# Moving the low parts of two kinds of weight tiles by 64 bytes, with the retention state updated in place

## The chip, the cores and the metric

One core of a Trainium2 chip runs the whole program. The metric is device time in microseconds (us) of one execution, taken as the median of several runs. Matrix products run on TensorE (PE in the profile, its weight loads PEld), elementwise work on VectorE (DVE) and ScalarE (ACT), a few small steps and some transfers on GpSimd (POOL); the other transfers are issued by SyncE (SP).

## What is computed

One decoder block over 512 tokens of width 1024, in float32. Two mixers work side by side on the normalised input: a chunked retention with 4 heads and a sliding-window attention with 8 heads. Their outputs are gated and merged, and a squared-ReLU MLP of width 4096 follows. Cut to what bears on the change:

```python
h = rmsnorm(x, pre_mix_norm)
q_r, k_r, v_r, g_r, q_s, k_s, v_s, gate_r, gate_s = split(h @ w_in)
# retention: 4 heads, chunks of 128 tokens; kv[n] = k_dec[n].T @ v[n] is 128 x 256
def step(s, kv_n): return chunk_decay * s + kv_n, s      # the state before each chunk
o = decayed(q k^T) v + q_dec @ s_prev                    # then normalised per head
y_r = (silu(g_r) * ret) @ w_ret_out
...
x = x + rmsnorm((sigmoid(gate_r) * y_r + sigmoid(gate_s) * y_s) @ w_out)
x = x + rmsnorm(relu(rmsnorm(x) @ w_up) ** 2 @ w_down)
```

## The kernel before

**Two-part operands.** Every large product is made from operands split in two: `split` writes the high part `hi` on ScalarE (L158, a cast to float32r) and the low part `lo = src - hi` on VectorE (L160). `mm3` then issues three matmuls for one product: high by high (L221), high by low (L222), low by high (L223). In a matmul one operand is loaded as weights (128 columns, the stationary one) while the other streams past it (256 or 512 columns, the moving one). In the text a triple is one `mm3`, and its time is from the start of its L221 to the start of the next triple's L221.

**Where the parts of a weight tile lie.** `place` (L165) hands out the high part as a slice of a tile of 1024 + 64 numbers, four in rotation: with `front=True` from its start, otherwise from its 16th number (64 bytes) on. The low part is a tile of its own, `wlo`, of 1024 numbers, and does not know `front`. The callers with `front=True` are `block_parts` (the q and k weights of retention heads 0 and 2, which are not computed in pairs) and `moving_parts` (the wide weights `w_v` and `w_g` of `wide`). As the pools lay it out in the built program, the starts in SBUF leave these remainders on division by 256 bytes. They are places of tiles, not measurements:

| operands of the triples | moving operand | stationary operand |
|---|---|---|
| `wide` before | `whi` 64, `wlo` 128 | `hT`, `hsum` 64 |
| `wide` after | `whi` 64, `wlo` 64 | `hT`, `hsum` 64 |
| plain retention blocks `pblk<-hT` before | `hT` 64 | `whi` 64, `wlo` 128 |
| plain retention blocks `pblk<-hT` after | `hT` 64 | `whi` 64, `wlo` 64 |
| `ps` (w_out), `yr`, `ys`, `p`, `pblk<-xg`, and the short `p4c`, before and after | 128 | 128 |
| `wino`, `up`, `rpair`, before and after | 64 | 128 |
| `ret_v<-st`, before and after | 64 | 64 |

No matmul other than those of the first two pairs of rows changes its remainders.

**Stages.** After the attention's queries come the q and k of head 0 (`ret_block`, `pblk`), then `wide(w_v)`: seven products of 8 triples each (2 token halves by 4 rows), interleaved with the attention's scores (`swa_s`), transposes (`psd`, `psp`) and values (`pso`). Then the four retention heads: a head's keys and scores, three states (`ret_st`, `ret_states`), the next head's q and k (`pblk` for head 2, a Winograd-like `rpair` for heads 1 and 3), and `ret_values`, in which chunk c needs state c - 1. The last head runs inside `wide(w_g)`, seven products more. Output projections, gates and the MLP follow.

**Retention state.** `ret_states` keeps the running state in a tile `st` of a rotation of two. The first state is a copy by ScalarE (L627), each later one is `prev * decay + kv` on VectorE (L629), written to the other tile, and each is split into a high and a low part by L158 and L160.

**What sets the order.** Each engine runs its own instructions in a fixed order, which a scheduler derives from the order of the code, from what depends on what and from `issue_after`, which holds steps back behind a named one. A tile of a rotation is handed out again once its last reader is done. The `accpool` tile `acc` (4096 numbers in each partition, one in rotation) first holds the two halves of `w_v` that `wide_sums` loads (L698, L700 on SP's queue, L699 on POOL's).

Of the kernel before, what the change touches and what calls it, by code (L numbers as in the profile page):

```python
# [10 lines left out]
F32 = mybir.dt.float32  # L11
F32R = mybir.dt.float32r
# [4 lines left out]
P = 128  # L17
D_MODEL = 1024
SEQ = 512
NT = SEQ // P  # L20
KD = D_MODEL // P
RET_HEADS = 4
RET_DK = 128
RET_DV = 256
# [19 lines left out]
def log_gammas():  # L44
    return np.log(1.0 - np.exp2(-5.0 - np.arange(RET_HEADS, dtype=np.float64)))
# [64 lines left out]
def block_kernel(ctx, tc, x, xT, pre_mix, w_in, w_qk, w_v, w_g, w_gate, w_ret, w_swa, w_out, sinks, post_mix,  # L110
# [6 lines left out]
    stream = ctx.enter_context(tc.tile_pool(name="stream", bufs=4))  # L117
    psum = ctx.enter_context(tc.tile_pool(name="psum", bufs=8, space=PSUM))
    small = ctx.enter_context(tc.tile_pool(name="small", bufs=4))

    def bank(shape, name="ps"):
        return psum.tile(shape, F32, tag="ps", name=name)

    def pad(pool, size, name="pad"):

        pool.tile([P, size // 4], F32, name=name, bufs=1)
# [18 lines left out]

    def rstd_of(sumsq, n, scale):

        ms = small.tile([P, 4], F32, name="ms", bufs=2)
        r = small.tile([P, 4], F32, name="rstd")
        nc.vector.tensor_scalar(ms[:, :n], sumsq, scale, EPS, op0=ALU.mult, op1=ALU.add)  # L150
        nc.gpsimd.tensor_tensor(r[:, :n], ms[:, :n], mhalf[:, :n], op=ALU.pow)
        return r

    last = {}

    def split(hi, lo, src):

        last["hi"] = nc.scalar.copy(hi, src)  # L158
        last["prior"] = last.get("split")
        last["split"] = nc.vector.tensor_tensor(lo, src, f(hi), op=ALU.subtract)  # L160
# [1 line left out]
    def raw_tile(shape):  # L162
        return stream.tile(shape, F32, name="raw", tag="raw", bufs=2)

    def place(shape, front=False):  # L165

        whole = stream.tile([P, 1024 + 64], F32R, name="whi", tag="whi")
        flat = whole[:, :1024] if front else whole[:, 16 : 16 + 1024]
        dims = " ".join("abc"[: len(shape) - 1])
        sizes = {n: shape[i + 1] for i, n in enumerate("abc"[: len(shape) - 1])}  # L170
        hi = flat.rearrange(f"p ({dims}) -> p {dims}", **sizes)
        if "wlo" not in last:
            pad(stream, 64)
            last["wlo"] = True
        return hi, stream.tile(shape, F32R, name="wlo", tag="wlo")

    def parts(src, shape, front=False):
        hi, lo = place(shape, front)
        split(hi, lo, src)
        return hi, lo  # L180

    def load_feature_pair(w, c0):

        nk = w.shape[0] // P
        raw = raw_tile([P, nk, 256])
        nc.sync.dma_start(raw, w[:, c0 : c0 + 256].rearrange("(k p) c -> p k c", p=P))
        return [parts(raw[:, :, b * P : (b + 1) * P], [P, nk, P]) for b in range(2)]
# [8 lines left out]
    def block_parts(raw):  # L196

        return [parts(raw[:, b], [P, KD, P], True) for b in range(2)]
# [19 lines left out]
    def mm3(ps, a, b, first, last, more=False):  # L218

        (ah, al), (bh, bl) = a, b  # L220
        nc.tensor.matmul(ps, ah, bh, start=first, stop=False, skip_group_check=more)  # L221
        nc.tensor.matmul(ps, ah, bl, start=False, stop=False, skip_group_check=more)  # L222
        return nc.tensor.matmul(ps, al, bh, start=False, stop=last, skip_group_check=more)  # L223
# [131 lines left out]
    accpool = ctx.enter_context(tc.tile_pool(name="accpool", bufs=1))  # L355
# [21 lines left out]
    xpool = xctx.enter_context(tc.tile_pool(name="xpool", bufs=1))  # L377
# [46 lines left out]
    def token_factors(t):  # L424

        ss = small.tile([P, 2], F32, name="ss", tag="ss", bufs=2)
        junk = xpool.tile([P, D_MODEL], F32, name="junk")
        last["square"] = nc.scalar.activation(junk, xts[t], AF.Square, accum_out=ss[:, 0:1])
        rstd[t] = rstd_of(ss[:, 0:1], 1, 1.0 / D_MODEL)[:, 0:1]
        diag[t] = xpool.tile([P, P], F32, name="diag", bufs=NT)  # L430
        nc.vector.tensor_scalar(diag[t], ident, rstd[t], None, op0=ALU.mult)
# [28 lines left out]
        return R  # L460

    def half_parts(src):
        hi, lo = place([P, KD, P])
        for i in range(2):
            k = slice(i * KD // 2, (i + 1) * KD // 2)
            split(hi[:, k], lo[:, k], src[:, k])
        return hi, lo

    wq = [half_parts(raw_q[:, :, :P]), parts(raw_q[:, :, P:], [P, KD, P])]
    for t in range(NT):  # L470
        token_factors(t)
# [140 lines left out]
    def ret_states(kd, v, h):  # L612

        decayed = float(np.exp(log_gammas()[h] * P))
        states, prev, pss = [], None, []
        for c in range(NT - 1):
            pss.append(bank([P, RET_DV], "ret_st"))
            mm3(
                pss[c], tuple(a[:, c, :] for a in kd), tuple(a[:, c, :] for a in v), True, True
            )  # L620
        for c in range(NT - 1):
            if c == 1:
                yield states
            st = [rpool.tile([P, RET_DV], F32R, name=f"st{i}", bufs=3) for i in range(2)]
            cur = rpool.tile([P, RET_DV], F32, name="st")
            if prev is None:
                nc.scalar.copy(cur, pss[c])  # L627
            else:
                nc.vector.scalar_tensor_tensor(  # L629
                    cur, prev, decayed, pss[c], op0=ALU.mult, op1=ALU.add  # L630
                )
            split(st[0], st[1], cur)
            states.append(st)
            prev = cur
        yield states
# [173 lines left out]
    rpool = rctx.enter_context(tc.tile_pool(name="rpool", bufs=2, side="right"))  # L809
# [57 lines left out]
    for i in range(3):  # L867
# [4 lines left out]
        if i == 1:  # L872
            rs = dpool.tile([P, 2, 4, P], F32, name="rs1", tag="qs")
# [12 lines left out]
    for h in range(RET_HEADS):  # L886
        if 0 < h < RET_HEADS - 1:
            wqk = load_qk(h + 1)
        with ExitStack() as queue:
            if h and h not in PAIRED:  # L890
                queue.enter_context(tc.issue_after(last["block"].ins))
            v = parts(vg[:, :, h * RET_DV : (h + 1) * RET_DV], [P, NT, RET_DV])
# [209 lines left out]
    for bp in range(KD // 2):  # L1102
# [3 lines left out]
        for b in range(2):  # L1106
            hi = mpool.tile([P, SEQ], F32R, name="mhi", tag="m")
            lo = mpool.tile([P, SEQ], F32R, name="mlo", tag="m")
# [20 lines left out]
    def square_sum(srcs, junk):  # L1129
        ss = small.tile([P, 2], F32, name="ss2", tag="ss", bufs=2)  # L1130
        for i, s in enumerate(srcs):
            c = slice(i * 512, (i + 1) * 512)
            nc.scalar.activation(junk[:, c], s, AF.Square, accum_out=ss[:, i : i + 1])
        nc.vector.tensor_add(ss[:, 0:1], ss[:, 0:1], ss[:, 1:2])
        return rstd_of(ss[:, 0:1], 1, 1.0 / D_MODEL)

    h2 = []
    for half in range(2):
# [11 lines left out]
        with tc.high_priority(offset=CHAIN_AHEAD):  # L1150
            for t in range(2):
# [4 lines left out]
                for n in range(2):  # L1156
                    c = slice(n * 512, (n + 1) * 512)
# [110 lines left out]
    dpool2 = ctx.enter_context(tc.tile_pool(name="dpool2", bufs=1, side="right"))  # L1268
# [92 lines left out]
    fin = ctx.enter_context(tc.tile_pool(name="fin", bufs=2))  # L1361
# [44 lines left out]
    def squares(t, i, src):  # L1406

        w = src.shape[1]
        junk = junks.tile([P, 512], F32, name="junk2")
        ss = fin.tile([P, 1], F32, name="ssf", bufs=6)  # L1410
        nc.scalar.activation(junk[:, :w], src, AF.Square, accum_out=ss)
        ms = fin.tile([P, 1], F32, name="msf", bufs=6)
        rest = EPS if i == 0 else ms0[t][:, 0:1]
        nc.vector.tensor_scalar(ms, ss, 1.0 / D_MODEL, rest, op0=ALU.mult, op1=ALU.add)
        ms0[t] = ms
# [14 lines left out]
    def weigh(n, src):  # L1430
        nc.vector.tensor_tensor(src, src, g_out[:, n * 512 : (n + 1) * 512], op=ALU.mult)


    for tb in range(2):
        nc.scalar.copy(p1c[tb], p1[tb])
        v = fin.tile([P, 512], F32, name="c", bufs=4)
        nc.vector.tensor_tensor(v, p2[tb], p1c[tb], op=ALU.add)
        squares(tb, 0, v)
        weigh(0, v)
        outz[tb] = v  # L1440
        nc.vector.tensor_tensor(p15[tb], p1c[tb], p5[tb], op=ALU.add)
    p6, p3 = banks2("p6"), banks2("p3")
    p7 = None
    rb = {}

    def step_p6(j):
        if j >= T2_DMA:
            nc.vector.tensor_tensor(tch[j], tch[j], rb[j], op=ALU.add)
        a, b = left(j, 1), right(tch[j])
        t_add(tch[j], 1, 0, j)  # L1450

        nc.vector.tensor_tensor(uc[j][:, 1], uc[j][:, 2], uc[j][:, 1], op=ALU.subtract)
        product2(p6, j, a, b)
# [22 lines left out]
    def combine(tb):  # L1476
        nc.vector.tensor_tensor(p15[tb], p6[tb], p15[tb], op=ALU.subtract)
        nc.vector.tensor_tensor(u3[tb], p6[tb], p1c[tb], op=ALU.subtract)
        nc.vector.tensor_tensor(p1c[tb], p3[tb], p15[tb], op=ALU.add)
        squares(tb, 1, p1c[tb])  # L1480
        nc.vector.tensor_tensor(u3[tb], p7[tb], u3[tb], op=ALU.add)
        v = fin.tile([P, 512], F32, name="c", bufs=4)
        nc.vector.tensor_tensor(v, p7[tb], p15[tb], op=ALU.add)
        squares(2 + tb, 0, v)
        outz[2 + tb] = v
# [24 lines left out]
    for i in range(2):  # L1510
        c = slice(i * 256, (i + 1) * 256)
# [9 lines left out]
    junk = junks.tile([P, 512], F32, name="junk2")  # L1521
    ms = fin.tile([P, 1], F32, name="msf", bufs=6)
# [43 lines left out]
```

## Time and profile before

| | |
|---|---|
| median of 3 runs | 713.01 us (712.79 to 713.19) |
| the profiled execution, its own time | 713.18 us |
| its span in the profile | 711.4 us |
| TensorE busy | 703.4 us, 4526 matmuls |
| VectorE, ScalarE, GpSimd busy | 535.4, 431.4, 62.3 us |

TensorE is busy for nearly the whole span, but a busy matmul in these records overlaps the next one: a matmul of 512 columns lasts 0.39 us in its row, and the next starts some 0.23 us after it. What a matmul costs is therefore read from the distance of starts, and over many matmuls, since a row's start is given to 0.01 us.

### The profile page before, as it was taken

To read this page: it belongs to the slowest core of one execution; us is meant where nothing else is said; L and a number is where in the kernel's file an instruction comes from. 1 tells how busy PE (TensorE), PEld (TensorE's weight loads), DVE (VectorE), ACT (ScalarE), POOL (GpSimd) and SP (SyncE) were. 2 spreads that over 40 slices of the span, in tenths; PEclk is the share of its full clock that TensorE was granted. 3 is DMA by queue.
4 is the path that set the end of the run, shared out by engine and by line. 5 is a ranking of instruction groups with operands and counts; after the bars stand their busy time and mean duration, and the time that the engine had idled before them with its cause. 6 is when DMAs were issued, how large, how long until landed. Compare 5 with 4: busy or idle time off the path is not lost.

```text
span 711.4 us, 11459 instructions
## 1 busy us (share of the span) xinstructions
PE 703.4 (99%) x4526; PEld 629.8 (89%) x4526; DVE 535.4 (75%) x801; ACT 431.4 (61%) x734; POOL 62.3 (9%) x78
## 2 busy tenths in 40 slices
PE   9999999999999999999999999999999999999996
PEld 9887889898888999989888999999999888888885
DVE  5699978685975767566945867778777887977797
ACT  6758776566655535435633866766668656655561
POOL 0300100121100000000011100000000100010010
PEclk9999999999999999999999999999999999999999
DMA  9974624876444545553661619777753999798603
GB/s 305 340 191 96 146 56 152 219 170 127 88 149 119 147 120 166 159 150 117 219 256 61 163 45 294 198 195 173 195 148 119 267 290 269 161 214 188 118 1 118
DMA packets 40613, 119.37 MB, mean 168 GB/s; under 512 B 3568, under 2 KB 17008, under 8 KB 34416
## 3 DMA queue, kind: packets, MB, share of 16 engines
q1 hardware_dynamic: 33648, 81.41, 33.0%
q0 software_dynamic: 6768, 37.23, 28.1%
q8 instruction: 35, 0.57, 0.3%
q14 instruction: 18, 0.15, 0.1%
q10 hardware_dynamic: 144, 0.00, 0.0%
HBM read 116.54 MB, written 2.10 MB: 167 GB/s over the span
## 4 chain that ended last, share of the span: by engine, by line
PE 91%; DVE 4%; DMA 2%; issue 1%; ACT 1%; SPq 0%; POOL 0%; DVEq 0%; POOLq 0%; ACTq 0%
PE wino L221 9%; PE wino L223 9%; PE wino L222 9%; PE p L221 5%; PE p L223 5%; PE p L222 5%; PE wide L221 4%; PE wide L222 4%; PE wide L223 4%; PE pblk L223 2%; PE pblk L222 2%; PE pblk L221 2%; PE yr L222 2%; PE ps L222 2%; PE ps L221 2%; PE yr L223 2%
## 5 line engine op out<-in xcount | busy, mean ns | idle before, releaser
L160 DVE TENSOR_TENSOR wlo<-raw,whi 128x1024 fp32r<-128x1024 f32 (+1 forms) x78 | 94.0, 1208 | 37.0 <-ACT whi L158 36.9
L158 ACT CAST whi<-raw 128x1024 fp32r<-128x1024 f32 (+1 forms) x78 | 80.6, 1039 | 19.5 <-PE p L223 4.6
L221 PE MATMUL p<-whi,left 128*128 128x512 f32 x216 | 84.0, 390 | 0.1
L222 PE MATMUL p<-wlo,left 128*128 128x512 f32 x216 | 84.1, 389 | 0.0
L223 PE MATMUL p<-whi,left 128*128 128x512 f32 x216 | 84.0, 390 | 0.0
L223 PEld LDWEIGHTS p<-whi,left 128*128 128x128 f32 x216 | 40.5, 188 | 8.7 <-DVE left L160 0.3
L222 PEld LDWEIGHTS p<-wlo,left 128*128 128x128 f32 x216 | 40.5, 188 | 8.6
L221 PEld LDWEIGHTS p<-whi,left 128*128 128x128 f32 x216 | 40.5, 188 | 8.6 <-ACT left L158 0.5
L158 ACT CAST p<-rs 128x1024 fp32r<-128x1024 f32 x22 | 23.1, 1052 | 36.5 <-DVE rs L275 36.4
L158 ACT CAST left<-uc 128x1024 fp32r<-128x1024 f32 x28 | 29.5, 1052 | 24.5 <-PE p L222 22.7
L160 DVE TENSOR_TENSOR left<-uc,left 128x1024 fp32r<-128x1024 f32 x28 | 34.2, 1221 | 12.3 <-ACT left L158 12.3
L160 DVE TENSOR_TENSOR p<-rs,p 128x1024 fp32r<-128x1024 f32 x22 | 27.0, 1225 | 16.7 <-ACT p L158 16.7
L160 DVE TENSOR_TENSOR wlo<-rs,whi 128x1024 fp32r<-128x1024 f32 x23 | 28.1, 1223 | 13.1 <-ACT whi L158 10.6
L158 ACT CAST whi<-acc 128x1024 fp32r<-128x1024 f32 x20 | 20.5, 1053 | 14.7 <-PE pblk L222 5.6
L221 PE MATMUL wino<-h2s,p 128*128 128x256 f32 x104 | 28.8, 277 | 0.0
L222 PE MATMUL wino<-h2s,p 128*128 128x256 f32 x104 | 28.7, 276 | 0.0
L223 PE MATMUL wino<-h2s,p 128*128 128x256 f32 x104 | 28.7, 276 | 0.0
L221 PE MATMUL wino<-h2c,whi 128*128 128x256 f32 x104 | 28.7, 276 | 0.0
L222 PE MATMUL wino<-h2c,whi 128*128 128x256 f32 x104 | 28.7, 276 | 0.0
L221 PE MATMUL wino<-h2s,whi 128*128 128x256 f32 x104 | 28.7, 276 | 0.0
L222 PE MATMUL wino<-h2s,whi 128*128 128x256 f32 x104 | 28.7, 276 | 0.0
L223 PE MATMUL wino<-h2s,wlo 128*128 128x256 f32 x104 | 28.7, 276 | 0.0
(413 smaller groups left out, 2373.0 us busy)
## 6 DMA issues: line engine op xcount, KB each, us to landing
rs<-in_w_up SPq DMA_DIRECT2D x13, 512.0 KB, 4.4
rs<-in_w_up POOLq DMA_DIRECT2D x13, 512.0 KB, 5.6
raw<-in_w_up SPq DMA_DIRECT2D x13, 512.0 KB, 5.5
tch<-in_w_down POOLq DMA_DIRECT2D x6, 1024.0 KB, 8.4
rd<-in_w_down SPq DMA_DIRECT2D x6, 1024.0 KB, 10.8
raw<-in_w_down POOLq DMA_DIRECT2D x6, 1024.0 KB, 11.5
acc<-in_w_v POOLq DMA_DIRECT2D x4, 1024.0 KB, 8.0
rs<-in_w_gate SPq DMA_DIRECT2D x8, 512.0 KB, 3.8
```

Of the source, the lines that this page charges most:

```text
L158: last["hi"] = nc.scalar.copy(hi, src)
L160: last["split"] = nc.vector.tensor_tensor(lo, src, f(hi), op=ALU.subtract)
L221: nc.tensor.matmul(ps, ah, bh, start=first, stop=False, skip_group_check=more)
L222: nc.tensor.matmul(ps, ah, bl, start=False, stop=False, skip_group_check=more)
L223: return nc.tensor.matmul(ps, al, bh, start=False, stop=last, skip_group_check=more)
```

## The change

`place` now makes one part at a time and is called for the high and for the low part, so that the low parts get tiles of 1024 + 64 numbers in four rotations of their own and obey `front`. Room in SBUF for them comes from four edits: the square's scratch tile `junk` moves from `xpool` into the one `acc` tile; the retention state is one tile for each head that is updated in place; the last products keep two of four `c` tiles in `dpool2` (`c2`); `ms` gets the pool's four tiles in place of two.

```diff
-        ms = small.tile([P, 4], F32, name="ms", bufs=2)
+        ms = small.tile([P, 4], F32, name="ms")
...
-    def place(shape, front=False):
-
-        whole = stream.tile([P, 1024 + 64], F32R, name="whi", tag="whi")
+    def place(name, shape, front=False):
+
+        whole = stream.tile([P, 1024 + 64], F32R, name=name, tag=name)
         flat = whole[:, :1024] if front else whole[:, 16 : 16 + 1024]
...
-        if "wlo" not in last:
-            pad(stream, 64)
-            last["wlo"] = True
-        return hi, stream.tile(shape, F32R, name="wlo", tag="wlo")
...
     def parts(src, shape, front=False):
-        hi, lo = place(shape, front)
+        hi, lo = place("whi", shape, front), place("wlo", shape, front)
         split(hi, lo, src)
...
-        junk = xpool.tile([P, D_MODEL], F32, name="junk")
+        if "junk" not in last:
+            last["junk"] = accpool.tile([P, D_MODEL], F32, name="junk", tag="acc")
+        junk = last["junk"]
...
     def half_parts(src):
-        hi, lo = place([P, KD, P])
+        hi, lo = place("whi", [P, KD, P]), place("wlo", [P, KD, P])
...
             st = [rpool.tile([P, RET_DV], F32R, name=f"st{i}", bufs=3) for i in range(2)]
-            cur = rpool.tile([P, RET_DV], F32, name="st")
+            cur = prev or rpool.tile([P, RET_DV], F32, name="st", bufs=1)
...
-        v = fin.tile([P, 512], F32, name="c", bufs=4)
+        v = fin.tile([P, 512], F32, name="c", bufs=2)
...
+    c2 = dpool2.tile([P, 2, 512], F32, name="c2", tag="rs")
...
-        v = fin.tile([P, 512], F32, name="c", bufs=4)
+        v = c2[:, tb]
```

No instruction is added or removed, and TensorE's order is the same. VectorE's and ScalarE's orders change around the retention states. On VectorE, head 0 (the tile `st` is the running state, `st_1338`, `st_1387` and `st_1393` are the low parts of the three states, `whi` and `wlo` from `vg` are the next head's values) stands before as:

```order
L629 SCALAR_TENSOR_TENSOR st<-st,ret_st 128x256
L160 TENSOR_TENSOR st_1338<-st,st_1337 128x256
L629 SCALAR_TENSOR_TENSOR st<-st,ret_st 128x256
L160 TENSOR_TENSOR swaT<-pso,swaT 128x512
L160 TENSOR_TENSOR st_1387<-st,st_1386 128x256
L160 TENSOR_TENSOR st_1393<-st,st_1392 128x256
L847 TENSOR_TENSOR qk<-rpair,qk 128x256
L848 TENSOR_TENSOR qk<-qk,rpair 128x256
L160 TENSOR_TENSOR wlo<-vg,whi 128x1024
```

and after (lines 2 less; `st_1334`, `st_1383`, `st_1388` are the low parts):

```order
L160 TENSOR_TENSOR st_1334<-st,st_1333 128x256
L627 SCALAR_TENSOR_TENSOR st<-st,ret_st 128x256
L160 TENSOR_TENSOR swaT<-pso,swaT 128x512
L160 TENSOR_TENSOR st_1383<-st,st_1382 128x256
L627 SCALAR_TENSOR_TENSOR st<-st,ret_st 128x256
L845 TENSOR_TENSOR qk<-rpair,qk 128x256
L846 TENSOR_TENSOR qk<-qk,rpair 128x256
L160 TENSOR_TENSOR wlo<-vg,whi 128x1024
L160 TENSOR_TENSOR st_1388<-st,st_1387 128x256
```

Each update of the state now stands behind the split of the state before it, and the third state's low part behind the wide split `wlo<-vg`. On VectorE, head 1 (`rs` and `p` are sums of the weights of head 3) before:

```order
L160 TENSOR_TENSOR st_1555<-st,st_1554 128x256
L629 SCALAR_TENSOR_TENSOR st<-st,ret_st 128x256
L275 TENSOR_TENSOR rs<-rs,raw 128x512
L160 TENSOR_TENSOR st_1561<-st,st_1560 128x256
L160 TENSOR_TENSOR p_1651<-rs,p_1650 128x1024
L160 TENSOR_TENSOR p_1655<-raw,p_1654 128x512
```

and after:

```order
L271 TENSOR_TENSOR rs<-rs,raw 128x512
L160 TENSOR_TENSOR st_1549<-st,st_1548 128x256
L627 SCALAR_TENSOR_TENSOR st<-st,ret_st 128x256
L160 TENSOR_TENSOR p_1643<-rs,p_1642 128x1024
L160 TENSOR_TENSOR st_1554<-st,st_1553 128x256
L160 TENSOR_TENSOR p_1647<-raw,p_1646 128x512
```

Here, too, the third state's low part has moved behind a wide split, that of `rs` into `p`. Heads 2 and 3 show the same move. SP's order is unchanged; its load of `acc` (L698) now waits for the last use of `junk` on ScalarE.

## Rows read from the trace of the kernel before

**Rows 1.** The page: granted clock in 40 slices; chain that ended last, by engine.
```profile
PEclk9999999999999999999999999999999999999999
...
PE 91%; DVE 4%; DMA 2%; issue 1%; ACT 1%; SPq 0%; POOL 0%; DVEq 0%; POOLq 0%; ACTq 0%
```

**Rows 2.** Timeline of PE, `wide` on `w_g`: start us, us, what.
```profile
173.27 0.39 PE L221 MATMUL wide<-whi,hT 128*128 128x512 f32 x1
...
173.97 0.39 PE L221 MATMUL wide<-whi,hT 128*128 128x512 f32 x1
...
174.65 0.40 PE L221 MATMUL wide<-whi,hT 128*128 128x512 f32 x1
...
176.04 0.40 PE L221 MATMUL wide<-whi,hT 128*128 128x512 f32 x1
...
176.75 0.39 PE L221 MATMUL wide<-whi,hT 128*128 128x512 f32 x1
...
201.10 0.39 PE L221 MATMUL ys<-swaT,whi 128*128 128x512 f32 x1
```

**Rows 3.** Timeline of PE, output projection `ps`, first and last start of 56 triples.
```profile
347.13 0.39 PE L221 MATMUL ps<-wo,mhi 128*128 128x512 f32 x1
...
385.21 0.40 PE L221 MATMUL ps<-wo,mhi 128*128 128x512 f32 x1
```

**Rows 4.** Timeline of PE, plain retention blocks of head 0.
```profile
41.16 0.39 PE L221 MATMUL pblk<-hT,whi 128*128 128x512 f32 x1
...
41.62 0.40 PE L223 MATMUL pblk<-hT,wlo 128*128 128x512 f32 x1
41.86 0.39 PE L221 MATMUL pblk<-hT,whi 128*128 128x512 f32 x1
...
51.56 0.39 PE L221 MATMUL pblk<-hT,whi 128*128 128x512 f32 x1
```

**Rows 5.** Timeline of PE, short triples (256 columns) of three stages.
```profile
110.88 0.28 PE L221 MATMUL rpair<-hT,whi 128*128 128x256 f32 x1
...
115.30 0.28 PE L221 MATMUL rpair<-hT,early_qk 128*128 128x256 f32 x1
...
125.23 0.28 PE L221 MATMUL ret_v<-st,qc 128*128 128x256 f32 x1
...
125.59 0.28 PE L221 MATMUL ret_v<-whi,pt 128*128 128x256 f32 x1
...
700.26 0.28 PE L221 MATMUL p4c<-whi,left 128*128 128x256 f32 x1
...
703.86 0.28 PE L221 MATMUL p4c<-whi,left 128*128 128x256 f32 x1
```

**Rows 6.** Timeline of DVE and PE around the third states of heads 0 and 1.
```profile
124.37 1.23 DVE L160 TENSOR_TENSOR wlo<-vg,whi 128x1024 fp32r<-128x1024 f32 x1 [0.20 <-ACT whi L158]
...
126.79 0.28 PE L222 MATMUL ret_v<-st,qc 128*128 128x256 f32 x1
...
139.84 0.42 DVE L160 TENSOR_TENSOR st<-st,st 128x256 fp32r<-128x256 f32 x1
...
141.04 1.22 DVE L160 TENSOR_TENSOR p<-rs,p 128x1024 fp32r<-128x1024 f32 x1 [0.78 <-ACT p L158]
...
142.63 0.28 PE L222 MATMUL ret_v<-st,qc 128*128 128x256 f32 x1
```

**Rows 7.** Timeline of DVE and PE where the attention's probabilities are handed over.
```profile
64.83 1.08 DVE L542 TENSOR_SCALAR s<-s,den 128x128 f32<-128x128 f32 x4
...
66.07 0.60 PE L554 MATMUL psd<-ident,s 128*128 128x128 f32 x4
```

**Rows 8.** Timeline of ACT and SP around the first load of `acc`.
```profile
21.95 1.06 ACT L428 ACTIVATE junk<-xt 128x1024 f32<-128x1024 f32 x1 [0.17 <-DMA xt<-in_x]
...
21.70 3.09 SPq L698 DMA_DIRECT2D acc<-in_w_v x1
...
36.47 1.06 ACT L158 CAST whi<-acc 128x1024 fp32r<-128x1024 f32 x1
```

More of the change, by code (lines that the diff above doesn't have):

```diff
@@ L163, in raw_tile @@
         return stream.tile(shape, F32, name="raw", tag="raw", bufs=2)
-    def place(shape, front=False):
-        whole = stream.tile([P, 1024 + 64], F32R, name="whi", tag="whi")
+    def place(name, shape, front=False):
+        whole = stream.tile([P, 1024 + 64], F32R, name=name, tag=name)
         flat = whole[:, :1024] if front else whole[:, 16 : 16 + 1024]
-        dims = " ".join("abc"[: len(shape) - 1])
-        sizes = {n: shape[i + 1] for i, n in enumerate("abc"[: len(shape) - 1])}
-        hi = flat.rearrange(f"p ({dims}) -> p {dims}", **sizes)
-        if "wlo" not in last:
-            pad(stream, 64)
-            last["wlo"] = True
-        return hi, stream.tile(shape, F32R, name="wlo", tag="wlo")
+        dims = "abc"[: len(shape) - 1]
+        sizes = {n: shape[i + 1] for i, n in enumerate(dims)}
+        return flat.rearrange(f"p ({' '.join(dims)}) -> p {' '.join(dims)}", **sizes)
     def parts(src, shape, front=False):
-        hi, lo = place(shape, front)
+        hi, lo = place("whi", shape, front), place("wlo", shape, front)
         split(hi, lo, src)
```

## The prediction

> **What bounds the kernel now.** I read first the slices of the granted clock and the shares of the chain that ended last [rows 1]. The clock is at its upper level of 2.4 GHz in every slice, so nothing is to be had from it, and 91% of the chain is TensorE: what ends last is nearly always the matmul before. Then I read the timeline of TensorE itself. A matmul's own duration (0.39 us) says little, because the next one starts long before it ends; the distance of starts is the cost. For 512 columns I formed it for whole triples, over long stretches in which no other instruction stands between.
>
> - Output projection, every operand at remainder 128: 56 triples from 347.13 to 385.21, 38.08 us, so 0.680 us a triple [rows 3].
> - `wide`, moving operands at 64, 128, 64 and stationary ones at 64: 40 triples from 173.27 to 201.10, 27.83 us, so 0.6958 us [rows 2]. The single triples are not equal: the one at 173.97 takes 0.68 us, the one at 176.04 takes 0.71, and after 5 triples (173.27 to 176.75, 3.48 us) the pattern begins again.
> - Plain retention blocks, moving operand at 64, stationary at 64, 64, 128: 15 triples from 41.16 to 51.56, 10.40 us, so 0.6933 us. Inside a triple, L221 and L222 together take 0.46 us, and L223, the one with the low part at 128, takes 0.24 [rows 4].
>
> So three groups with the same shapes and the same clock cost differently, the cheapest being the one whose three matmuls have all operands at one remainder. The two dearer groups are those that the change touches, and in each of them one matmul in three has a mixed pair.
>
> **The change part by part.** *The wide triples.* There are 14 products of 8 triples, 112. If they come to the cost of the uniform triples, each gives back 0.6958 - 0.6800 = 0.0158 us, together 1.77 us. *The plain blocks.* Heads 0 and 2 have two blocks of 8 triples each, 32 triples; each gives back 0.0133 us, together 0.43 us. The sum is 2.2 us. The trace of before has no 512-column triple with all operands at 64, so the value rests on the uniform ones at 128 [rows 3]. The bounds: at best 0.678 us, since the cheap step of the wide pattern is 0.68 as well and rows are given to 0.01 us [rows 2], which makes 2.5 us; at worst the dearest step of that pattern, 0.71 us, for every triple, which is a loss (below). I take the uniform price because a shift of all operands by the same 64 bytes leaves their distance as it is, and the distance is what differs between the groups.
>
> *Where the gain could be stopped.* A faster TensorE runs into whatever is handed to it late. In most of this stretch operands are ready some microseconds early. The tight place is the attention's first probabilities: VectorE ends them at 64.83 + 1.08 = 65.91 us, and the fourth transpose of the group that starts at 66.07 follows three others at about 0.11 us each, near 66.40 [rows 7]. Up to there TensorE would be 16 x 0.0133 + 16 x 0.0158 = 0.47 us ahead, against 0.49 us of room less the handover. I charge 0.1 us, between none and the whole 0.47. Behind it the scores and their splits on VectorE wait for TensorE and move with it. Net gain: 2.1 us.
>
> *The retention states in place.* No instruction is added; three of them in each head swap places on VectorE and ScalarE. TensorE needs the third state's low part at the last L222 of `ret_v`: 126.79 us in head 0, 142.63 in head 1 [rows 6]. In head 0 that part now stands behind `wlo<-vg`, which ends at 124.37 + 1.23 = 125.60; with the split's 0.42 us it is there at about 126.05, 0.7 us early. In head 1 it stands behind the split of `rs` into `p` (1.22 us). There the first update has moved behind the first sum of `rs` and the second update behind the other, so the sums that `p` waits for come about 0.4 us sooner (one such step), and `p` starts near 140.65 in place of 141.04; 140.65 + 1.22 + 0.42 is about 142.3, 0.3 us early. Before, that state's split began at 139.84. Queued behind the late splits are the norm's statistics, which are not needed at once. I put it at nothing: the cover is 0.3 to 0.7 us in a head, and if it is gone, each head can lose what exceeds it, at most about one wide split, 1.2 us. Below nothing I see no way.
>
> *The scratch tile.* SP's load of `acc` was issued at 21.70 us; it now waits for the last square on ScalarE, which begins at 21.95 and takes 1.06 us, so it goes out at about 23.1, 1.4 us later [rows 8]. Behind it on SP stand the second half of `acc` and the small tables; POOL's addition waits for its landing. ScalarE first reads `acc` at 36.47 us. The issue itself took 3.09 us, which I take for a full queue: the earlier loads were still running, and a later entry into a full queue need not land later. Even 1.4 us more is covered, since the first product on these weights is a dozen microseconds behind that read. Cost nothing, at most 0.2 us. The `ms` and `c` tiles change no wait on the path: nothing.
>
> *The sum.* 713.18 us of the profiled execution less 2.1 us is 711.1; the median of the runs was 0.17 us lower than that execution, so I forecast 710.9 us.
>
> Here a rule speaks against the change. The Trainium skill, "SBUF — State Buffer", section "Who interferes with whom", gives TensorE two independent read ports, one for the moving operand and one for weight loads, and says that "PE and ACT never wait on anyone." By that rule a start address could not change a triple's time, and the sum would be 713.0 us. The rows disagree with it as far as they go: 0.680 us against 0.6958 and 0.6933 for the same work, and 0.24 against 0.23 us for neighbouring matmuls of one triple.
>
> **The rivals.** *The remainder is not the cause.* The dearer triples also differ in what runs beside them, since `wide` is interleaved with attention work and states. If that is what sets the 0.6958, the moved tiles change nothing and the time stays at 713.0 us. Against it: the five-triple pattern repeats without regard to what ScalarE and VectorE do, and in the plain blocks the dear matmul is always the one with the low part [rows 2, 4]. Chance 0.14.
>
> *A half gain.* In the plain blocks L221 and L222 have all operands at 64 and take 0.46 us a pair, 0.23 each, where 0.680 / 3 is 0.227 [rows 3, 4]. At some 0.685 us a triple the gain is 112 x 0.0108 + 32 x 0.0083 = 1.5 us less 0.1, so 711.6 us. Chance 0.12.
>
> *Uniform, but dear: slower.* For short triples equal remainders are the expensive case. Ten `p4c` triples, all at 128, take 3.60 us, 0.360 each, and a `ret_v` triple, all at 64, takes 0.36; 13 `rpair` triples at 64 against 128 take 4.42 us, 0.340 each [rows 5]. If equal starts at 64 hold a long triple in the dear step of the wide pattern, 0.708 us, the loss is 112 x 0.012 + 32 x 0.015 = 1.8 us: 714.8 us. It decides from a mean triple above 0.696 us. Against it: equal remainders of 128 are the cheapest of the long triples. Chance 0.07.
>
> *A wait takes the gain.* The third state's split comes too late in each of the four heads, by about 0.8 us each: 3.2 us lost against 2.1 gained, 714.1 us. For it: only 0.3 us of room in head 1. Against it: the wide split ahead does not wait for anything new. Chance 0.05.
>
> **How the numbers follow.** Forecast 710.9 us with chance 0.62, its own range 710.4 to 711.5. The lower end adds to it that some 36 short triples of the retention stage, which take up to 0.36 us, may fall to 0.340 as the order of starts shifts, 0.5 us. For all cases together 8 in 10 need the range to reach up to no change, 713.0; that leaves out the two slower rivals (0.12), part of the unchanged case and a little below. About 0.2% (1.4 us) is what a measurement of this kernel can tell from no change. Faster by more than that, under 711.6: the forecast and half of the half gain, 0.68. Within it: the other half and the unchanged case, 0.20. Slower: 0.12.
>
> **What would show it.** In the profile of the changed kernel 40 `wide` triples without anything between them should take 27.2 us in place of 27.83, with equal steps of 0.68 and no pattern of five, and the 15 plain triples 10.2 in place of 10.40. TensorE's rows from `ys` on should stand some 2.1 us earlier, by about 0.2 us already at `swa_s`. The third state's low part should be seen near 126 and 142 us with no gap in front of the last `ret_v` triple. I am wrong if the wide triples keep their 0.696, if the gain at `ys` is not there at the end, or if TensorE waits for `st`.

## The result and the profile after

The changed kernel takes 711.95 us (median of 15 runs, 711.48 to 712.34) where the kernel before, run beside it, takes 713.23 us (15 runs, 712.74 to 714.17): 0.9982 of the time, with a 95% interval of 0.9975 to 0.9989, or 1.28 us less. A second set of runs of the same two kernels gave 711.21 against 712.98 us, 0.9976 [0.9967, 0.9986], 1.77 us less. The two intervals overlap; between them the gain is some 1.5 us, about 0.2%. The profiled execution of the changed kernel took 711.96 us, with a span of 710.2 us where before had 711.4. The first profile of either kernel is read here unless another is named; times of groups of matmuls are summed from the distances of starts.

The page answers [rows 1] with the same picture, apart from the clock's last slice, where the kernel before with the state edit alone shows the same 8 at an unchanged time; the first line is the granted clock in 40 slices, the second the chain by engine:

```profile
PEclk9999999999999999999999999999999999999998
...
PE 92%; DVE 4%; DMA 2%; issue 1%; ACT 1%; POOL 0%; SPq 0%; DVEq 0%; POOLq 0%; ACTq 0%
```

The timeline of TensorE over `wide` on `w_g` (start us, us, what) answers [rows 2]:

```profile
172.30 0.39 PE L217 MATMUL wide<-whi,hT 128*128 128x512 f32 x1
...
172.98 0.39 PE L217 MATMUL wide<-whi,hT 128*128 128x512 f32 x1
...
182.50 0.39 PE L217 MATMUL wide<-whi,hsum 128*128 128x512 f32 x1
...
183.24 0.50 PE L217 MATMUL wide<-whi,hsum 128*128 128x512 f32 x1
...
184.05 0.40 PE L217 MATMUL wide<-whi,hsum 128*128 128x512 f32 x1
...
184.74 0.39 PE L217 MATMUL wide<-whi,hsum 128*128 128x512 f32 x1
...
199.69 0.39 PE L217 MATMUL ys<-swaT,whi 128*128 128x512 f32 x1
```

These are the same 40 triples. The first 15 (172.30 to 182.50) take 10.20 us and the last 22 (184.74 to 199.69) take 14.95, which is 0.680 us each; the pattern of five is gone. Between them stand three that take 0.74, 0.81 and 0.69 us: a new wait. So the 40 take 27.39 us, against 27.83 before. `ys` starts 1.41 us earlier than before, at 199.69 for 201.10; 0.19 us of that is no gain of the change, since TensorE's rows stand that much earlier already at 17 us, behind its first products (`ptok`).

The plain blocks of head 0, the same view, for [rows 4]:

```profile
40.98 0.39 PE L217 MATMUL pblk<-hT,whi 128*128 128x512 f32 x1
...
41.45 0.39 PE L219 MATMUL pblk<-hT,wlo 128*128 128x512 f32 x1
41.68 0.39 PE L217 MATMUL pblk<-hT,whi 128*128 128x512 f32 x1
...
51.20 0.39 PE L217 MATMUL pblk<-hT,whi 128*128 128x512 f32 x1
```

The matmul with the low part takes 0.23 us to the next start, 0.24 before. The 15 triples take 10.22 us (40.98 to 51.20), 10.40 before: 0.70 for the first and 14 at 0.680.

Summed over the whole program, from before to after, and in a second profile of the changed kernel (`after_again` below), in us:

| part | before | after | after_again |
|---|---|---|---|
| 112 triples of `wide` | 79.17 | 77.91 | 77.81 |
| 32 triples of the plain blocks | 22.34 | 22.02 | 22.04 |
| 12 triples of `ret_st` | 4.39 | 4.50 | 4.51 |
| 28 triples of `ret_v` | 10.00 | 10.08 | 10.04 |
| `rpair` | 19.52 | 19.68 | 19.55 |

That is 1.59 and 1.67 us gained in the long triples and 0.36 and 0.19 us given back in the short ones. What else differs between two profiles of one kernel is mostly its two ends: the span of `after_again` is 0.9 us shorter than that of the first, of which 0.4 us stand before 17 us and 0.3 behind 650 us.

**Which triples gained.** In the first profile 81 of the 112 `wide` triples run at 0.680 us; these same triples took 56.39 us before and 55.08 now, 0.0162 us each. The other 31 took 22.79 and take 22.83. They are the first one to four behind each interruption by transposes, short products or a wait (0.797, then 0.691, 0.697 and 0.684 us at 53.69 to 55.87 us, where before had 0.797, 0.697, 0.696 and 0.701), the last ones ahead of the next, and the three at 183 us. Of the 32 plain triples 25 run at 0.680 and give 0.33 us; the other seven give nothing. A stretch of TensorE behind an interruption thus comes to the cheap pace one to four triples after its start: in the stretches at 84.6 and 100.9 us already the second triple takes 0.680.

**The new wait.** ScalarE and VectorE at 183 us (columns as above, idle time before and its releaser in brackets):

```profile
182.08 0.63 ACT L952 ACTIVATE vg<-vg 128x512 f32<-128x512 f32 x1 [0.89 <-DVE retn L951]
182.62 0.57 ACT L742 COPY vg<-wide 128x512 f32<-128x512 f32 x1
...
181.36 0.69 DVE L951 TENSOR_TENSOR retn<-retn,vg 128x512 f32<-128x512 f32 x1
```

The `wide` chain's bank must be copied out (L742) before TensorE adds the next product to it. That copy stands on ScalarE behind a sigmoid, and the sigmoid waits for VectorE's product (L951), which ends at 182.05. The copy ends at 183.19, and TensorE's next product begins at 183.24. ScalarE had waited idle for 0.89 us ahead of the sigmoid. The same two rows of before, the copy and the first matmul of the next product:

```profile
183.34 0.57 ACT L744 COPY vg<-wide 128x512 f32<-128x512 f32 x1
...
184.41 0.39 PE L221 MATMUL wide<-whi,hsum 128*128 128x512 f32 x1
```

There the copy ended at 183.91, 0.50 us ahead of the product. TensorE now comes to this place 1.17 us earlier and ScalarE's copy only 0.72, which uses up the cover. In `after_again` the same three triples lose 0.10 us and not 0.19; the size of the wait differs between executions.

**The short triples.** In `ret_st` TensorE runs into VectorE once, at the third state of head 0. The rows of after, then of before, VectorE's with the bank's last read, then TensorE's:

```profile
116.75 0.41 DVE L838 TENSOR_TENSOR qk<-rpair,qk 128x256 f32<-128x256 f32 x1
...
117.22 0.39 PE L217 MATMUL ret_st<-whi,kd 128*128 128x256 f32 x1
117.44 0.28 PE L218 MATMUL ret_st<-wlo,kd 128*128 128x256 f32 x1
```

```profile
117.66 0.41 DVE L840 TENSOR_TENSOR qk<-rpair,qk 128x256 f32<-128x256 f32 x1
...
118.22 0.28 PE L221 MATMUL ret_st<-whi,kd 128*128 128x256 f32 x1
118.35 0.28 PE L222 MATMUL ret_st<-wlo,kd 128*128 128x256 f32 x1
```

VectorE's row has moved 0.91 us, TensorE's 1.00, and the matmul now holds the next one off for 0.22 us where it was 0.13. Of all that was gained up to there 0.1 us stays in this place; that the bank is what it waits for is inferred from these rows.

### The profile page after: what moved, and what is told of

It is laid out like the page before. It is cut to its first block, busy times and chain, and to the rows that moved or that the text cites. A ratio compares the mean times of both kernels' runs of the same rounds, so it can differ in the third digit from the quotient of the medians.

```text
span 710.2 us, 11455 instructions
## 1 busy us (share of the span) xinstructions
PE 702.1 (99%) x4526; PEld 629.7 (89%) x4526; DVE 535.5 (75%) x801; ACT 431.4 (61%) x734; POOL 62.1 (9%) x78
## 4 chain that ended last, share of the span: by engine, by line
PE 92%; DVE 4%; DMA 2%; issue 1%; ACT 1%; POOL 0%; SPq 0%; DVEq 0%; POOLq 0%; ACTq 0%
PE wino L217 9%; PE wino L219 9%; PE wino L218 9%; PE p L217 5%; PE p L218 5%; PE p L219 5%; PE wide L217 4%; PE wide L218 4%; PE wide L219 4%; PE pblk L219 2%; PE pblk L217 2%; PE pblk L218 2%; PE yr L218 2%; PE yr L217 2%; PE ps L217 2%; PE ps L218 2%
## 5 line engine op out<-in xcount | busy, mean ns | idle before, releaser
L158 ACT CAST whi<-rd 128x1024 fp32r<-128x1024 f32 x18 | 18.9, 1050 | 16.4 <-PE p L219 9.4
L219 PE MATMUL wino<-h2c,wlo 128*128 128x256 f32 x104 | 28.7, 276 | 0.0
L217 PE MATMUL wino<-h2s,whi 128*128 128x256 f32 x104 | 28.7, 276 | 0.0
```

## The experiments

Each set of runs had its own runs of the kernel before, and a ratio is to those: 713.03 us (33 runs) for the first four kernels below; 712.72 (27) for the copy ahead of the sigmoid, the added matmul, the moved short triples and the first set of the three edits together; 712.98 (20) for the two kernels run once more (`after_again`, `before_again`) and the second set of the three edits.

**The remainders undone.** All else of the change stays, the low parts go back to 128:

```diff
-        hi, lo = place("whi", shape, front), place("wlo", shape, front)
+        hi, lo = place("whi", shape, front), place("wlo", shape)
```

> The changed kernel with one part undone: the low parts always start 64 bytes into their tile, so every matmul has the remainders of before, while the state in place, the scratch tile in acc and the order of all engines stay as changed. If the remainders alone bring the gain: wide triples go back to 0.696 us in their pattern of five, plain blocks to 0.693. If the state in place costs something of its own (short retention triples at 0.353 in place of 0.340), the time is above the kernel before, 713.4 to 713.6 us; if it costs nothing, 713.2; if the gain came from the other edits, it stays at 712.0.

Measured 712.96 us, 1.0 [0.9991, 1.0008]. The 40 triples (TensorE's timeline, first and last row):

```profile
173.22 0.39 PE L217 MATMUL wide<-whi,hT 128*128 128x512 f32 x1
...
201.05 0.39 PE L217 MATMUL ys<-swaT,whi 128*128 128x512 f32 x1
```

27.83 us, to the hundredth what [rows 2] give. All 112 together take 79.17 us, as before. The whole gain, then, comes from the starts of the low parts, and the other edits bring neither gain nor a loss that the times show.

**The state in place alone**, in the kernel before:

```diff
-            cur = rpool.tile([P, RET_DV], F32, name="st")
+            cur = prev or rpool.tile([P, RET_DV], F32, name="st", bufs=1)
```

> The kernel before with one part of the change alone: the retention state is one tile for each head, updated in place. If this edit by itself moves the short retention triples to the dearer step, 713.5 us (0.3 over before) with rpair, ret_st and ret_v together 0.3 us longer; if those short triples only follow the starts that the cheaper wide triples shift, no difference, 713.2 us.

Measured 713.06 us, 0.9999 [0.999, 1.0008]. Nothing is lost that could be measured, and not the 0.3 us that the first reading expected. Its trace shows 0.16 us more in `rpair` (19.68), which alone would look like a price of the edit; `after_again` below says otherwise.

**Distance 64, with both moving parts alike.** The wide weights' high and low parts both at 128, against stationary operands at 64:

```diff
-        tiles = [parts(raw[:, :h, :], [P, h, width], True)]
+        tiles = [parts(raw[:, :h, :], [P, h, width])]
...
-            tiles.append(parts(raw[:, h:, :], [P, h, width], True))
+            tiles.append(parts(raw[:, h:, :], [P, h, width]))
```

> The changed kernel with high and low parts of the wide weights both at remainder 128, against stationary operands at 64. If a triple is cheap only when moving and stationary operands have one remainder: wide triples of 0.696 us or more, the time 713.2 us or more. If it is enough that the two moving parts have the same remainder: 0.680 us and 712.0 us.

**Distance 128**, by the same lines with an offset of 32 numbers, both parts at 192 against 64:

```diff
...
-        flat = whole[:, :1024] if front else whole[:, 16 : 16 + 1024]
+        flat = whole[:, front : front + 1024]
...
-            tiles.append(parts(raw[:, h:, :], [P, h, width], True))
+            tiles.append(parts(raw[:, h:, :], [P, h, width], 32))
```

> As the run with both moving parts at 128, but at 192, 128 bytes from the stationary operands. One remainder needed: 0.69 us a triple or more, 712.9 us or more. Same remainder of the two moving parts enough: 0.680 us and 712.0 us. A price that grows with the distance would show as a triple dearer than at 128.

Measured 712.30 us, 0.9991 [0.9982, 1.0], and 712.69 us, 0.9994 [0.9985, 1.0002]; neither time can be told from before with certainty, so the triples decide. The 40 of the first, then of the second:

```profile
172.79 0.40 PE L217 MATMUL wide<-whi,hT 128*128 128x512 f32 x1
...
200.79 0.39 PE L217 MATMUL ys<-swaT,whi 128*128 128x512 f32 x1
```

```profile
172.97 0.40 PE L217 MATMUL wide<-whi,hT 128*128 128x512 f32 x1
...
200.97 0.40 PE L217 MATMUL ys<-swaT,whi 128*128 128x512 f32 x1
```

Both take 28.00 us, 0.700 each, which is dearer than before. At distance 64 each of these triples takes 0.700; in the earlier stretches, up to 170 us, the same kernel holds 0.687, as in these 12 triples (56.28 to 64.52, 8.24 us):

```profile
56.28 0.39 PE L217 MATMUL wide<-whi,hT 128*128 128x512 f32 x1
...
64.52 0.39 PE L217 MATMUL wide<-whi,hsum 128*128 128x512 f32 x1
```

At distance 128 they alternate, 0.704 and 0.696. All 112 take 78.86 and 79.47 us, where before had 79.17 and the changed kernel 77.91. That the parts agree with each other is therefore not enough; they must agree with the stationary operand. The forecast times, 713.2 and 712.9 us or more, were too high all the same: the plain blocks, unchanged in both, keep 22.02 to 22.04 us and with them 0.3 us of the gain, and at distance 64 the triples of 0.687 are cheaper than the mean of before. In the 40 triples the mean does not grow from distance 64 to 128; over all 112 it does, by 0.005 us a triple.

**The copy ahead of the sigmoid**, in the changed kernel: one pair of ScalarE's instructions exchanged, so that the copy no longer stands behind the sigmoid.

```diff
-            nc.scalar.copy(c(0, 1, tb), chain[tb])
+            last["c01"] = nc.scalar.copy(c(0, 1, tb), chain[tb])
+            last.setdefault("c01s", []).append(last["c01"])
...
-        nc.scalar.activation(g, g, AF.Sigmoid)
+        with ExitStack() as queue:
+            if not i and t == 1:
+                queue.enter_context(tc.issue_after(last["c01s"][-2].ins))
+            nc.scalar.activation(g, g, AF.Sigmoid)
```

> The changed kernel with two neighbours on ScalarE exchanged: the copy of the wide chain (issued at 182.62 us) stands ahead of the sigmoid that waits for VectorE's product (182.08 us). Theory: that sigmoid held up the copy, and TensorE waited for the copy at 182.50 to 183.24 us (triples of 0.75 and 0.80 us); the first triples there come back to 0.68 and about 0.70 us, 0.15 to 0.2 us less at 185 us and at ys, 711.8 us in the median. Rival: TensorE waited there for the next split (a low part on VectorE): the two triples stay at 0.75 and 0.80 us, 711.95 us.

Measured 711.18 us, 0.998 [0.9971, 0.9988]. Its timelines of ScalarE and TensorE:

```profile
180.74 0.58 ACT L742 COPY vg<-wide 128x512 f32<-128x512 f32 x1
181.73 0.63 ACT L956 ACTIVATE vg<-vg 128x512 f32<-128x512 f32 x1 [0.41 <-DVE retn L952]
...
172.24 0.39 PE L217 MATMUL wide<-whi,hT 128*128 128x512 f32 x1
...
182.44 0.39 PE L217 MATMUL wide<-whi,hsum 128*128 128x512 f32 x1
...
183.12 0.39 PE L217 MATMUL wide<-whi,hsum 128*128 128x512 f32 x1
...
199.44 0.39 PE L217 MATMUL ys<-swaT,whi 128*128 128x512 f32 x1
```

The copy is done at 181.32, the triples at 182.44 and 183.12 take 0.68 us, and all 40 take 27.20 us, 0.680 each. So the wait was ScalarE's queue, and in the first profile of the changed kernel it cost 0.19 us. Against the kernel before, the ratio is not distinguishable from the changed kernel's; the trace shows the gain, the times do not.

**An added short matmul ahead of the second half of the pair products**, in the changed kernel:

```diff
+            entry(p25[:, 1, :ENTRY], a["s3"][0][:, 0], b["t3"][0][:, 0, :ENTRY])
             wino_product(chain, a["s3"], b["t3"], False)
```

> The changed kernel with one matmul of 32 columns more, ahead of the second half of each head's pair products (its result is overwritten). Theory: a 256-column triple has two stable paces, 0.340 and 0.353 us, and where the stretch starts decides which; then the 12 triples of head 0 (119 to 124 us), which went from 0.340 to 0.353 with the change, and those of head 2 (150 to 154 us), can come out at 0.340 again: 0.16 us less for each half that changes its pace, less some 0.05 to 0.1 us for each added matmul, so 711.8 to 712.0 us, and the paces in the trace change. Rival: the pace is set by what VectorE and ScalarE do beside it; then both halves stay at 0.353 and the time is 712.0 to 712.2 us.

Measured 711.7 us, 0.9985 [0.9976, 0.9994]. The half at 119 us (head 0 in the text above) stayed at 0.353 us a triple. The one at 150 us (head 2) went to 0.340, in these rows of TensorE:

```profile
149.78 0.30 PE L301 MATMUL rpair<-hsum,whi 128*128 128x32 f32 x2
149.91 0.36 PE L217 MATMUL rpair<-hsum,whi 128*128 128x256 f32 x1
...
154.09 0.28 PE L217 MATMUL ret_v<-whi,pt 128*128 128x256 f32 x1
```

But the addition and the longer first matmul took more than it won: from 149.78 to 154.09 us is 4.31 us, where the changed kernel needs 4.24 (149.78 to 154.02) at the dear pace. No gain here.

**The changed kernel, and the one before, once more.** No edit.

> The changed kernel once more, unaltered. Theory: the pace of the second half of a head's pair products (12 triples of 256 columns at 0.340 or 0.353 us) is settled by the phase at which TensorE comes to it, which differs between executions of one program; then this profile may show 0.340 at 119 us where the first showed 0.353, and the state in place did not cause it. Rival: the order of the states on VectorE and ScalarE causes it; then it stays at 0.353. Median 711.4 to 711.9 us; the wide stretch at 172.79 to 200.1 us in triples of 0.680 us, a wait of 0.15 to 0.2 us at 183 us as before.

> The kernel before once more, unaltered, for the spread between two profiles of one program: 712.7 to 713.2 us. By the theory (phase) the second half of head 0 may show 0.353 us a triple where the first profile showed 0.340, 0.16 us more; by the rival (states in place cause 0.353) it shows 0.340 again. Wide triples 0.696 us in the mean.

Measured 711.21 us, 0.9976 [0.9967, 0.9986], and 713.04 us, 1.0 [0.9991, 1.0009]. TensorE's timeline over the second half of head 0's pair products, 12 triples, in the first profile of the changed kernel and in this one:

```profile
119.45 0.38 PE L217 MATMUL rpair<-hsum,whi 128*128 128x256 f32 x1
...
123.80 0.28 PE L217 MATMUL ret_v<-whi,pt 128*128 128x256 f32 x1
```

```profile
119.06 0.39 PE L217 MATMUL rpair<-hsum,whi 128*128 128x256 f32 x1
...
123.27 0.28 PE L217 MATMUL ret_v<-whi,pt 128*128 128x256 f32 x1
```

4.35 us and 4.21 us: behind a first triple of 0.46 us in both, the same program holds 0.353 us a triple once and 0.340 the other time. So neither the state in place nor any other edit settles the pace at this place. The kernel before showed 0.340 in both of its profiles, so that the change makes 0.353 likelier is not excluded; two profiles can't tell. The wait at 183 us came out at 0.10 us, under the 0.15 to 0.2 expected.

**The short triples of the states and values moved**, in the changed kernel: moving operands at 192, stationary ones at 0.

```diff
...
-            v = parts(vg[:, :, h * RET_DV : (h + 1) * RET_DV], [P, NT, RET_DV])
+            v = parts(vg[:, :, h * RET_DV : (h + 1) * RET_DV], [P, NT, RET_DV], 32)
...
+    for i in range(2):
+        rpool.tile([P, RET_DV], F32R, name=f"st{i}", bufs=3)
+    pad(rpool, 64)
...
+            pad(rpool, 64, "tail")
...
```

> The changed kernel with the operands of the retention states and values moved: moving ones at remainder 192, stationary ones at 0, where they were at 64 or 128 against 64. Theory: the distance of the two remainders decides, not the remainders themselves, and for 256 columns a stationary operand 64 bytes past the moving one is the cheap case (0.340 us at 64 against 128, rows of the pair products): 28 triples of ret_v fall from 0.356 to 0.365 us to 0.340, 0.56 us, and 12 of ret_st from 0.354 to 0.340, 0.17 us; together 0.7 us, 711.25 us. Rival A: these triples are dear because products of one or two triples follow one another and change bank: unchanged, 711.95 us. Rival B: they fall to 0.353 only: 0.2 to 0.3 us, 711.7 us.

Measured 710.88 us, 0.9972 [0.9962, 0.9981]. `ret_v` fell from 10.08 and 10.04 us to 9.90, its triples, 0.340 to 0.370 in the two profiles of the changed kernel, now all between 0.352 and 0.357; `ret_st` did not fall (4.54). The expected 0.340 did not come: Rival B, 0.353 only, is what `ret_v` shows, and a distance of 64 is not by itself the cheap case of short triples. The rest of what the trace shows is `rpair` at 0.340 in both second halves (19.37 us). In time, 1.84 us below the kernel before is not distinguishable from the 1.77 of the unaltered changed kernel.

**Three edits together**, in two sets of runs: the copy ahead of the sigmoid, the moved short triples, and, as the third, the moving operands of the last short products at 64 against 128:

```diff
...
-    ab = [(left(j, 3), right(tch[j])) for j in (2, 3)]
+    ab = [(left(j, 3), right(tch[j], True)) for j in (2, 3)]
```

> The changed kernel with both of the last two edits, and with the moving operand of the last short products (p4c, 16 triples of 0.360 us with all operands at 128) at 64 against 128. Theory: p4c falls to 0.340 us, 0.31 us less; the 8 long triples that share those operands rise from 0.680 to 0.687 to 0.700 us, 0.06 to 0.16 us more. With 0.7 us of the short triples and 0.19 us of the copy: 1.0 to 1.1 us less than the changed kernel, 710.9 us. Rival: p4c is dear because of its own place at the end (few products beside it): it stays at 0.360, and only the other two edits count, 711.1 us; if they fail too, 712.0 us.

> The kernel with all three further edits once more, beside the changed kernel: 0.7 to 1.0 us below it, 710.6 to 711.0 us; both second halves (119 and 149 us) at 0.340 us as in its first profile if the remainders of the states ahead of them settle the pace, at 0.353 in one of them if only the phase does.

Measured 710.60 us, 0.9972 [0.9961, 0.9983], and 710.70 us, 0.9969 [0.9957, 0.9982]. The last products in the first profile, 16 triples:

```profile
696.58 0.28 PE L218 MATMUL p4c<-whi,left 128*128 128x256 f32 x1
...
701.92 0.28 PE L220 MATMUL p4c<-whi,left 128*128 128x256 f32 x1
```

From the first start to the start of the last triple's last matmul 5.34 us; less the two matmuls of 0.11 us ahead of that one, 15 triples in 5.11 us, 0.341 each where [rows 5] show 0.360. That is 0.28 us. The same rows of the second profile:

```profile
696.25 0.28 PE L218 MATMUL p4c<-whi,left 128*128 128x256 f32 x1
...
701.79 0.28 PE L220 MATMUL p4c<-whi,left 128*128 128x256 f32 x1
```

Here it is 5.54 us, less two matmuls of 0.12 us 5.30, so 0.353 each, and only 0.09 us less than the changed kernel. Of the eight long triples on the same operands, those in steady pace rose from 0.680 to 0.700, as at distance 64 above.

In the second profile the pace of 0.353 appeared also in the first half of the pair products at 142 us, where no other profile had it, while both second halves had 0.340. So at three places (the halves at 119 and 142 us, the last products) one program shows either pace. The half at 150 us is different: it took 0.353 in all nine profiles without the added matmul and without the moved short triples, and 0.340 in all four with one of them. There an edit goes with the pace, so that the phase alone, which differs between executions, does not account for it. What settles a pace is not shown.

This kernel's medians are the lowest of all. In the set that has both it is 0.5 us below the changed kernel, less than the 0.7 to 1.0 expected, and the intervals overlap.

## Why the prediction was right, and where its sizes were off

Forecast was 710.9 us, or 2.1 us less; measured were 1.28 and 1.77 us less. The first median, 711.95 us, lies above the forecast's own range (710.4 to 711.5) and among the cases within 1.4 us of no change, which had a chance of 0.20; the second, 711.21, lies inside. The cause and its sign came out, the size was too large.

- *The remainder is the cause, and 0.680 us the price of a uniform triple*: right. Undone, all of the gain goes (712.96 us), and clean triples at 64 against 64 take 0.680 us as those at 128 against 128 do [rows 3]. The argument that a shift of all operands keeps their distance held, as far as distances of 0, 64 and 128 bytes tell: at 64 and 128 the price is 0.687 to 0.704.
- *112 wide triples by 0.0158 us, 1.77 us*: mis-sized, 1.26 us in the first profile and 1.36 in the second. A gain of 0.0162 us came in 81 of them, 1.31 us; the other 31 cost what they did, 0.05 us more in all. The rows of the prediction [rows 2] are from the longest stretch without interruption, and the price was laid on every triple, those behind transposes and short products too. Three of the 31 are the wait at 183 us, 0.19 us.
- *32 plain triples by 0.0133 us, 0.43 us*: the same error. 25 of them gave 0.33 us, the other seven nothing.
- *0.1 us where TensorE runs into VectorE*: the kind was right, the place wrong, and the size too small: 0.2 to 0.3 us were lost elsewhere. At the attention's probabilities TensorE did not wait. VectorE's and TensorE's rows there, for [rows 7]:

```profile
64.45 1.07 DVE L540 TENSOR_SCALAR s<-s,den 128x128 f32<-128x128 f32 x4
...
65.49 0.60 PE L552 MATMUL psd<-ident,s 128*128 128x128 f32 x4
```

VectorE ends at 65.52; the fourth transpose, three times 0.11 us behind 65.49, is near 65.82. The room shrank from 0.49 to 0.30 us. Instead, TensorE ran into others at 117 us (0.1 us, VectorE) and at 183 us (0.19 us in one profile, 0.10 in the other, ScalarE). The second was missed where operands were taken to be ready "some microseconds early": the text goes over VectorE's hand-overs and not over what stands in ScalarE's queue ahead of a bank's copy, where the rows of before had 0.50 us of cover.

- *The states in place at nothing, with a cover of 0.3 to 0.7 us*: right, with more cover. The third states, for [rows 6], VectorE's split and the matmul that needs it, of heads 0 and 1:

```profile
124.69 0.42 DVE L160 TENSOR_TENSOR st<-st,st 128x256 fp32r<-128x256 f32 x1
...
126.07 0.28 PE L218 MATMUL ret_v<-st,qc 128*128 128x256 f32 x1
...
140.12 0.42 DVE L160 TENSOR_TENSOR st<-st,st 128x256 fp32r<-128x256 f32 x1
...
141.83 0.28 PE L218 MATMUL ret_v<-st,qc 128*128 128x256 f32 x1
```

Ready at 125.11 and 140.54, needed at 126.07 and 141.83: about 1.0 and 1.3 us early. In the kernel before with this edit alone the time did not move.

- *Short triples that may fall to 0.340, up to 0.5 us, the lower end of the range*: not seen. They took 0.36 and 0.19 us more, 0.16 and 0.03 of it in `rpair`, whose pace differs between executions.

- *The scratch tile at nothing*: right. For [rows 8], SP's load and ScalarE's first read:

```profile
23.28 1.66 SPq L696 DMA_DIRECT2D acc<-in_w_v  x1
...
36.29 1.06 ACT L158 CAST whi<-acc 128x1024 fp32r<-128x1024 f32 x1
```

The load went out 1.6 us later than before, its issue took 1.66 us in place of 3.09, and it landed at 30.96 us where before had 30.90: as argued, the later entry did not land later, and the read was not late.

- *The rivals.* The remainder as no cause: refuted by the undone kernel. Uniform but dear: refuted, 0.680 us. The half gain named 711.6 us, which lies between the two measured medians, but by a triple of 0.685 us that no clean stretch shows; the time came near it for another reason. Late third states: not seen. The rule of the Trainium skill ("SBUF — State Buffer", "Who interferes with whom"), by which, as the prediction reads it, a start address could not matter to TensorE, would have given 713.0 us for this change; 712.96 us with the starts undone and 711.2 to 712.0 with them speak against it.

Together: 2.2 us were forecast in the long triples and 1.6 to 1.7 found there (the triples behind interruptions and the wait at 183 us are the missing 0.5 to 0.6), and 0.2 to 0.4 us were given back in short triples. That leaves 1.2 and 1.5 us in the two profiles, beside the 1.28 and 1.77 us of the medians.

What stays open: why the start addresses of the moving and the stationary operand act on each other at all; whether 256 bytes is the right divisor, since no run gave long triples a distance other than 0, 64 and 128; why one kernel holds 0.687 in one stretch and 0.700 in another; and what lets a stretch of short triples settle at 0.340 or at 0.353 us.

## What to carry to other kernels

Where the weights are loaded anew for every matmul, as here, try to let the moving and the stationary operand of long matmuls start at the same remainder. The cost of a distance shows in the distances of starts, as unequal steps where one matmul in three is mixed (0.68 to 0.71) or as an even 0.700, and hardly in a matmul's own duration (0.39 or 0.40 us in these rows, but for the one that waits at 183.24). Price such a gain only on triples in undisturbed stretches: count those behind each interruption out. Read the same program's profile twice before a few tenths of a microsecond are put down to an edit. Before charging where a faster engine will run into others, follow each bank's last reader in its own queue, and ask what stands ahead of it there.

## What was not expected of the hardware

- Triples of 512 columns have a price by the distance of the two starts: 0.680 us at equal remainders, 0.687 or 0.700 with both moving parts 64 bytes on, 0.704 and 0.696 in turn at 128 bytes. At 64 bytes the same kernel holds 0.687 in one stretch and 0.700 in another.
- For 256 columns it is the other way at the end of the program: 0.360 us at equal remainders in all eleven profiles that have them there, 0.341 and 0.353 at 64 against 128.
- Triples of 256 columns at 64 against 128 have two stable paces, 0.340 and 0.353 us, and at some places the same program takes the one or the other from execution to execution.
- Behind transposes or values of the attention the first triple of a stretch of `wide` costs about 0.8 us. The next three take 0.691, 0.697 and 0.684 before 0.680 holds in the stretch at 53.69 us, while at 84.6 and 100.9 us 0.680 holds from the second on.
